# Sparse attention with queries made transposed, a 96-row compressed-value product, and a reordered opening

## The chip, the cores and the metric

One core of a Trainium2 chip runs the kernel. Its engines have queues of their own: TensorE (PE, with its weight loads PEld), VectorE (DVE), ScalarE (ACT), GpSimd (POOL) and SyncE (SP, which here only issues loads). The metric is the time of one execution on the device in microseconds (us); lower is better.

## The reference

Two layers of a decoder on 256 tokens of width 1024, all in fp32. Layer 0 mixes with causal pooling and a gated delta rule, layer 1 with the sparse attention below; each layer then attends to 256 memory tokens and applies a squared-ReLU MLP.

```python
q, kc, vc, ks, vs, kw, vw, gl = split_cols(z, C_SIZES)      # z = rmsnorm(x) @ w_in
ck = compress_kv(kc, ...); cv = compress_kv(vc, ...)        # 15 compressed blocks, 4 groups of 64
...
p_cmp = where(any(ok_c), softmax(q . ck * scale - slope * dist), 0)
o_cmp = einsum('bgrqc,bcgd->bqgrd', p_cmp, cv)
...
o = gb[..., 0:1] * o_cmp + gb[..., 1:2] * o_slc + gb[..., 2:3] * o_win
```

There are 16 query heads of 64 columns in 4 groups; three branches (compressed, selected, window) with their own keys and values are mixed by sigmoid gates.

## The kernel before, in words

**Three-term products.** Every weight arrives in fp32 and is split by `wsplit`: ACT writes the high part `hi` (L187), DVE or POOL the rest `lo` (L188; after a step `sh2` every second split goes to POOL). Activations are split likewise by `evac_hl` (ACT L245 `hh`, DVE L247 or L249 `hl`). `mm3` then multiplies hi by hi, hi by lo and lo by hi (L197 to L199) in fp32r. `block_b` makes a 128-column block of the output transposed (weights stationary, 24 matmuls of 256 columns); `dense_a` makes it with tokens on the partitions (matmuls of up to 512 columns, activations stationary).

**The opening** is in `mixer0`: tokens in two tiles t of 128, the row norm (`norm_act`, `norm_dve`, `norm_pow` L394 and L395, `norm_mul` L399 and L400 writing `cv`), PE transposes (`flip`, L455) into four PSUM tiles `pt` that hold two of the eight blocks k each, their evacuation `evac_x`, and a first product `first_mm` on the weights `a_ba`. `ea` (L493) and `onh` (L494) are two small results from the constants `vec`. A manual schedule keeps this part in the order written.

**The order of the rest** is set by lists of steps (`MIX` for layer 0's mixer, `NSA` for the sparse attention), run one after the other; a scheduler with priorities then places each engine's instructions, and fills with the projections of the memory attention (`k0` to `k8`). In `MIX`, `inv0` and its followers invert 32x32 blocks: ACT copies blocks into `ec` (L598), DVE multiplies by masks (`al`, L605), forms `T` (L609) and transposes it into `bc` (L611), PE multiplies (`blocks32`, L592), ACT takes the result as `Y` (L623).

**The sparse attention** is `nsa`. Steps `q0` and `q1` are two `dense_a` of 512 query columns; `ev_q` scales by the row norm `r` and by a row of constants `qr0` or `qr1` (`qd`, L1143) and splits each head into high and low 64 columns (`qn`, ACT L1148, DVE L1149). Steps `t0` to `t3` transpose these (L1160) and copy them (`qs`, L1162), so that `qs` has a head's high part on partitions 0 to 63 and its low part on 64 to 127. `compress` multiplies by the compression weights (L1080), `s` or `pc` receives its result (L1084); `comp_k` (L1091) and `comp_v` (L1102, L1104) go on from it. Step `s` p (`scores`) treats two heads: products with `vw`-tagged keys (L1177 to L1187), softmax pieces on DVE (L1193, L1199 to L1204). Step `v` p (`values`) transposes the probabilities (L1217 for the compressed branch `Pc`, evacuated to `pcT` at L1218; L1227 to L1229 for the others) and accumulates: L1244 and L1246 on 64-column tiles, then the compressed branch:

```python
            pe.matmul(po[:, :S], CV[g][:64], pcT[:64], start=False, stop=True)
```

`CV` and `pcT` are fp32 there, 64 rows: two heads with 32 rows each, of which 15 hold blocks.

## Time and profile before

| | |
|---|---|
| three runs | 863.91, 864.16, 864.18 us (median 864.16) |
| the profiled execution | 865.69 us, its span 863.9 us |
| busy in the span | PE 847.2, PEld 766.0, DVE 534.3, ACT 500.9, POOL 202.9 us |
| the chain that ended last | PE 89%, DVE 4%, ACT 3% |

The span is the part of an execution that the profiler shows; the execution's own time holds what lies around it. A matmul's busy time counts its latency, and neighbours overlap, so the pitch from start to start says what one costs. Times in the rows are microseconds from the span's start.

### The profile page before, as it was taken

The numbers are of one execution on the slowest core, as the hardware profiler recorded it, in microseconds if no ns is written. First come the engines' busy times: TensorE is split into PE (matmuls) and PEld (weight loads), VectorE is DVE, ScalarE is ACT, GpSimd is POOL, SyncE is SP. The second block draws the span as 40 slices with busy tenths as digits, with TensorE's granted clock in tenths as the row PEclk, the third lists the DMA queues.
The fourth block names the chain that finished last, engine by engine and source line by source line (L and its number), as shares of the span: only waits on it lengthen the run. The fifth ranks groups of instructions, "written<-read, shape, count | busy, mean of one in ns | idle before, by whom it ended". The sixth has DMA issues, their size and how long they took to land.

```text
span 863.9 us, 16134 instructions
## 1 busy us (share of the span) xinstructions
PE 847.2 (98%) x6231; PEld 766.0 (89%) x6231; DVE 534.3 (62%) x1043; ACT 500.9 (58%) x1018; POOL 202.9 (23%) x185
## 2 busy tenths in 40 slices
PE   7999999999999999999999999999999999999997
PEld 5999998899899999999889888888998999999995
DVE  5897657566575555555548797855555755555554
ACT  5896655755475445445676667756554754554452
POOL 0001710400012222222334454443100122222220
PEclk9999999999999999999999999999999999999999
DMA  8643444465546666666644321145545466666641
GB/s 281 191 135 101 137 127 140 156 213 184 158 147 201 189 191 183 191 193 199 203 148 162 125 99 50 51 123 173 167 152 166 147 198 192 189 184 190 191 151 49
DMA packets 41261, 138.77 MB, mean 161 GB/s; under 512 B 4576, under 2 KB 5088, under 8 KB 41184
## 3 DMA queue, kind: packets, MB, share of 16 engines
q1 hardware_dynamic: 40032, 135.69, 50.6%
q10 hardware_dynamic: 1152, 2.05, 0.7%
q8 instruction: 49, 0.80, 0.4%
q14 instruction: 28, 0.23, 0.1%
HBM read 136.67 MB, written 1.05 MB: 159 GB/s over the span
## 4 chain that ended last, share of the span: by engine, by line
PE 89%; DVE 4%; ACT 3%; issue 1%; DMA 1%; SPq 0%; POOL 0%; POOLq 0%; DVEq 0%; ACTq 0%
PE acc L197 12%; PE acc L199 12%; PE acc L198 12%; PE mb L197 10%; PE mb L198 10%; PE mb L199 10%; PE tp L197 4%; PE tp L198 4%; PE tp L199 4%; PE acc L592 1%; PE tp L259 1%; PE tp L1244 1%; DVE lo L188 1%; ACT hi L187 1%; ACT junk L273 1%
## 5 line engine op out<-in xcount | busy, mean ns | idle before, releaser
L187 ACT ACTIVATE hi<-raw 128x1024 fp32r<-128x1024 f32 (+2 forms) x256 | 263.8, 1033 | 252.5 <-PE acc L199 116.8
L188 DVE TENSOR_TENSOR lo<-raw,hi 128x1024 fp32r<-128x1024 f32 (+3 forms) x227 | 277.6, 1225 | 195.4 <-ACT hi L187 194.3
L197 PE MATMUL acc<-hi,hh 128*128 128x512 f32 (+3 forms) x496 | 189.2, 382 | 0.0
L198 PE MATMUL acc<-lo,hh 128*128 128x512 f32 (+3 forms) x496 | 189.0, 381 | 0.0
L199 PE MATMUL acc<-hi,hl 128*128 128x512 f32 (+3 forms) x496 | 188.9, 381 | 0.0
L197 PE MATMUL mb<-hh,hi 128*128 128x256 f32 x640 | 182.1, 285 | 0.6 <-ACT hi L187 0.6
L198 PE MATMUL mb<-hl,hi 128*128 128x256 f32 x640 | 181.1, 284 | 0.0
L199 PE MATMUL mb<-hh,lo 128*128 128x256 f32 x640 | 180.1, 283 | 0.0
L946 POOL TENSOR_TENSOR rs<-rs 128x256 f32<-128x256 f32 x64 | 74.5, 1174 | 238.7 <-ACT rs L944 238.7
L197 PEld LDWEIGHTS mb<-hh,hi 128*128 128x128 f32 x640 | 120.7, 189 | 2.5 <-ACT hi L187 1.1
L198 PEld LDWEIGHTS mb<-hl,hi 128*128 128x128 f32 x640 | 120.9, 189 | 2.2 <-issue 1.0
L199 PEld LDWEIGHTS mb<-hh,lo 128*128 128x128 f32 x640 | 121.2, 190 | 0.1
L199 PEld LDWEIGHTS acc<-hi,hl 128*128 128x128 f32 x496 | 93.5, 189 | 18.4 <-DVE hl L249 0.6
L197 PEld LDWEIGHTS acc<-hi,hh 128*128 128x128 f32 x496 | 93.7, 189 | 17.5
L198 PEld LDWEIGHTS acc<-lo,hh 128*128 128x128 f32 x496 | 93.7, 189 | 17.2
L188 POOL TENSOR_TENSOR lo<-raw,hi 128x1024 fp32r<-128x1024 f32 (+2 forms) x29 | 68.8, 2373 | 93.1 <-ACT hi L187 86.5
L197 PE MATMUL tp<-hh,hi 128*128 128x256 f32 x256 | 72.0, 281 | 0.0
L198 PE MATMUL tp<-hl,hi 128*128 128x256 f32 x256 | 71.7, 280 | 0.0
L199 PE MATMUL tp<-hh,lo 128*128 128x256 f32 x256 | 71.6, 280 | 0.0
L199 PEld LDWEIGHTS tp<-hh,lo 128*128 128x128 f32 x256 | 48.3, 188 | 0.0
L198 PEld LDWEIGHTS tp<-hl,hi 128*128 128x128 f32 x256 | 48.2, 188 | 0.0
L197 PEld LDWEIGHTS tp<-hh,hi 128*128 128x128 f32 x256 | 48.1, 188 | 0.0
...
## 6 DMA issues: line engine op xcount, KB each, us to landing
raw<-in_ff_w_dram SPq DMA_DIRECT2D x128, 512.0 KB, 3.8
...
```

The costliest lines, as they stand in the source:

```text
L187: act.activation(hi[:, :n], raw[:, :n], AF.Copy)
L188: lo_eng.tensor_sub(lo[:, :n], raw[:, :n], f(hi[:, :n]))
L197: pe.matmul(ps, sh, mh, start=start, stop=False)
L198: pe.matmul(ps, sh, ml, start=False, stop=False)
L199: pe.matmul(ps, sl, mh, start=False, stop=stop)
L259: pe.transpose(ps[:, j * S + t * P:j * S + (t + 1) * P], src(t, k0 + j), ident)
L273: act.activation(junk[:, :src.shape[-1]], src, AF.Square, accum_out=accum)
L592: pe.matmul(ps[o, c], lhs[o, c], rhs[o, c], start=True, stop=True)
L946: pool.tensor_tensor(sq, rl, rl, op=ALU.mult)
L1244: pe.matmul(po[rows, :S], v, pts[a][bi][:, :S], start=bi == 0, stop=False)
```

## The change

Queries are made transposed at once: eight `block_b` of 128 columns (two heads) replace the two `dense_a`, the transposes and their copies. `ev_q` scales by a column `qcol` and by `rb`, the row norm along the columns (made by `r_cols` with two products and a copy), ACT writes the high part on the head's own 64 partitions and DVE the low part on the other 64. The compressed values become 96 rows in fp32r: three groups of 32 rows with high part, low part and high part of `CV`, against high, high and low part of `pcT`, one pass. `hp` and `Pc` are written in three copies for that. In the opening `ea` and `onh` come last, the eight blocks are evacuated in the order 0, 2, 1, 3, 4, 6, 5, 7, and the part has a higher priority. `MIX` and `NSA` list their steps in another order.

```diff
...
-NSA = """sh2 kcvc w0 kskw pre0 vs gate kb0 kb1 q0 pre1 vw kb2 ck kb3 t0 t1 s0 w1 k0 q1 cv s1 v0 k1 s2 k2 v1 v2 s3 k3
+NSA = """sh2 kcvc w0 kskw pre0 vs rb gate q0 kb0 kb1 q1 pre1 vw ck kb3 s0 k0 q2 w1 q3 cv kb2
...
-        with tc.manual_schedule(engines={mybir.EngineType.Activation, mybir.EngineType.DVE, mybir.EngineType.PE}):
+        with tc.high_priority(offset=1000), tc.manual_schedule(engines={mybir.EngineType.Activation, mybir.EngineType.DVE, mybir.EngineType.PE}):
...
-            def first_mm(j):
-                for k2 in range(2):
-                    k = 2 * j + k2
-                    h3, l3 = (b3(z[:, :528], 264) for z in us[j])
-                    for t in range(2):
-                        mm3(ps[t][:, :264], tuple(a[:, t * P:(t + 1) * P] for a in hT[k]), (h3[:, k2], l3[:, k2]), k == 0, k == KT - 1)
-            for j in range(4):
-                for k in (2 * j, 2 * j + 1):
+            def first_mm(k):
+                h3, l3 = (b3(z[:, :528], 264) for z in us[k // 2])
+                for t in range(2):
+                    mm3(ps[t][:, :264], tuple(a[:, t * P:(t + 1) * P] for a in hT[k]), (h3[:, k % 2], l3[:, k % 2]), k == 0, k == KT - 1)
+
+            for ks in ((0, 2), (1, 3), (4, 6), (5, 7)):
+                for k in ks:
                     evac_x(pt, k)
-                if j < 2:
-                    us.append(wsplit("a_ba", j + 2, 528))
-                first_mm(j)
+                    if k in (2, 3):
+                        us.append(wsplit("a_ba", k, 528))
+                    first_mm(k)
+            act.activation(ea, V("a_log"), AF.Exp)
+            dve.tensor_scalar(onh, V("o_norm"), 0.5, None, op0=ALU.mult)
...
-        act.activation(ea, V("a_log"), AF.Exp)
-        dve.tensor_scalar(onh, V("o_norm"), 0.5, None, op0=ALU.mult)
...
-        D1, Dc, qr0, qr1 = gt('D1', 1, 528), gt('Dc', 1, 400), gt('qd', 3), gt('qd', 3)
-        for d, o in ((D1, 0), (Dc, 528), (qr0, 928), (qr1, 1440)):
+        D1, Dc = gt('D1', 1, 528), gt('Dc', 1, 408)
+        for d, o in ((D1, 0), (Dc, 528)):
             nc.scalar.dma_start(d, A["cst2"][:, o:o + d.shape[-1]])
-        D0, cblk = Dc[:, :272], Dc[:, 272:]
+        D0, cblk, qcol = Dc[:, :272], Dc[:, 272:400], Dc[:, 400:]
...
-            hp = gt('pc', 2, 256)
+
+            hp = gt('z', 8)[:, :384]
             pool.memset(hp, 0.0)
-            hp4 = hp.rearrange("p (g a b) -> p g a b", g=4, a=2)
-            compress(1, pre[1], w1[1], [hp4[:, :, a, :15] for a in range(2)])
+            compress(1, pre[1], w1[1], [hp.rearrange("p (g c b) -> p g c b", g=4, c=6)[:, :, c, :15] for c in range(6)])
             ps = tp()
             for g in range(4):
-                pe.matmul(ps[:64, g * 64:(g + 1) * 64], hp[:, g * 64:(g + 1) * 64], V("w2_v"), start=True, stop=True)
-            cv = gt('cv', 1)
-            dve.tensor_tensor(cv[:64].rearrange("p (g a d) -> p g a d", g=4, a=2),
-                              b3(ps[:64, :256], 64).unsqueeze(2).to_broadcast([64, 4, 2, 64]),
-                              b3(cblk[:64], 64).unsqueeze(1).to_broadcast([64, 4, 2, 64]), op=ALU.mult)
+                pe.matmul(ps[:96, g * 64:(g + 1) * 64], hp[:, g * 96:(g + 1) * 96], V("w2_v"), start=True, stop=True)
+            cvf, cv = gt('z', 8), gt('cv', 1, 512, F32R)
+            dve.tensor_tensor(cvf[:96].rearrange("p (g a d) -> p g a d", g=4, a=2),
+                              b3(ps[:96, :256], 64).unsqueeze(2).to_broadcast([96, 4, 2, 64]),
+                              b3(cblk[:96], 64).unsqueeze(1).to_broadcast([96, 4, 2, 64]), op=ALU.mult)
+            act.activation(cv[:96], cvf[:96], AF.Copy)
+            dve.tensor_sub(cv[32:64], cvf[32:64], f(cv[32:64]))
             for g in range(4):
-                CV.append(cv[:, g * P:(g + 1) * P])
+                CV.append(cv[:96, g * P:(g + 1) * P])
...
-        Pc = [gt(f"Pc{i}", 1, P).rearrange("p (t a b) -> p t a b", t=2, a=2) for i in range(2)]
-        for z in Pc:
-            pool.memset(z, 0.0)
+        Pc = {}
 
         oT = [None] * 8
-        qn = {}
-
-        def ev_q(c):
-            def ev(t, q, ps):
-                d = gt('qd', 3)
-                dve.scalar_tensor_tensor(d, ps, r[:, t:t + 1], (qr0, qr1)[c], op0=ALU.mult, op1=ALU.mult)
-                for i in range(2):
-                    s = gt('qn', 4, 512, F32R)
-                    s4 = s.rearrange("p (h a d) -> p h a d", h=4, a=2)
-                    d3 = b3(d[:, i * 256:(i + 1) * 256], 64)
-                    act.activation(s4[:, :, 0], d3, AF.Copy)
-                    dve.tensor_sub(s4[:, :, 1], d3, f(s4[:, :, 0]))
-                    qn[2 * c + i, t] = s
-            return ev
-
         qs = {}
         ek = {}
-
-        def q_t(g):
+        rb = gt('rb', 1, S)
+
+        def r_cols():
+
+            ps = tp()
             for t in range(2):
-                ps = tp()
-                for h in range(4):
-                    pe.transpose(ps[:, h * P:(h + 1) * P], f(qn[g, t][:, h * P:(h + 1) * P]), ident)
-                qs[g, t] = gt('qs', 4, 512, F32R)
-                act.activation(qs[g, t], ps, AF.Copy)
+                pe.matmul(ps[:, t * P:(t + 1) * P], r[:, t:t + 1].to_broadcast([P, P]), ident, start=True, stop=True)
+            act.activation(rb, ps[:, :S], AF.Copy)
+
+        def ev_q(p, ps):
+
+            d = gt('qd', 3, S)
+            dve.scalar_tensor_tensor(d, ps, qcol[:, p:p + 1], rb, op0=ALU.mult, op1=ALU.mult)
+            s = gt('qs', 8, 512, F32R)
+            u, v = slice(0, 64), slice(64, 128)
+            for rows, other, c in ((u, v, slice(0, S)), (v, u, slice(S, 2 * S))):
+                act.activation(s[rows, c], d[rows], AF.Copy)
+                dve.tensor_sub(s[other, c], d[rows], f(s[rows, c]))
+            qs[p] = s
...
-            pc = Pc[p % 2]
+            pc = small([P, 2, 2, 16], "pcp", 2)
             for t in range(2):
                 for a in range(2):
-                    h = (2 * p + a) % 4
-                    st = qs[g, t][:, h * P:(h + 1) * P]
+                    st = qs[p][:, a * S + t * P:a * S + (t + 1) * P]
...
-            pc = pc[:, :, :, 0:16]
...
-            dve.tensor_tensor(pc, pc, rs[:, :, :, 0:1].to_broadcast([P, 2, 2, 16]), op=ALU.mult)
+            Pc[p] = gt('Pc', 2, 192).rearrange("p (t c a b) -> p t c a b", t=2, c=3, a=2)
+            for t in range(2):
+                dve.tensor_tensor(Pc[p][:, t], pc[:, t].unsqueeze(1).to_broadcast([P, 3, 2, 16]),
+                                  rs[:, t, :, 0:1].unsqueeze(1).to_broadcast([P, 3, 2, 16]), op=ALU.mult)
...
-            pcT = gt('pc', 2, 256)[:, :S]
+            pcT = gt('pc', 2, S, F32R)
             ps = tp()
             for t in range(2):
-                pe.transpose(ps[:64, t * P:(t + 1) * P], Pc[p % 2][:, t].rearrange("p a b -> p (a b)"), ident)
-            act.activation(pcT[:64], ps[:64, :S], AF.Copy)
+                pe.transpose(ps[:96, t * P:(t + 1) * P], Pc[p][:, t].rearrange("p c a b -> p (c a b)"), ident)
+
+            act.activation(pcT[:96], ps[:96, :S], AF.Copy)
+            dve.tensor_sub(pcT[64:96], ps[64:96, :S], f(pcT[64:96]))
...
-            pe.matmul(po[:, :S], CV[g][:64], pcT[:64], start=False, stop=True)
+            pe.matmul(po[:, :S], CV[g], pcT[:96], start=False, stop=True)
...
```

ACT's queue in the opening, before (`junk` are the sums of squares, `cv` the normalised tokens, `hi` the split of `a_ba`, `hh` the evacuated blocks; `tp_136` and `tp_137` are two PSUM tiles):

```order
L493 ACTIVATE ea_360<-vec 128x4
L400 ACTIVATE cv_124<-x_83,n_0_8_127 128x512
L187 ACTIVATE hi_158<-raw_93 128x528
L400 ACTIVATE cv_126<-x_85,n_0_8_127 128x512
L187 ACTIVATE hi_172<-raw_93 128x528
L245 ACTIVATE hh_178<-tp_136,vec 128x256
L245 ACTIVATE hh_182<-tp_136,vec 128x256
L187 ACTIVATE hi_186<-raw_97 128x528
L245 ACTIVATE hh_202<-tp_137,vec 128x256
L245 ACTIVATE hh_206<-tp_137,vec 128x256
```

and now:

```order
L400 ACTIVATE cv_124<-x_83,n_0_8_127 128x512
L187 ACTIVATE hi_159<-raw_93 128x528
L400 ACTIVATE cv_126<-x_85,n_0_8_127 128x512
L187 ACTIVATE hi_173<-raw_93 128x528
L245 ACTIVATE hh_179<-tp_137,vec 128x256
L245 ACTIVATE hh_189<-tp_138,vec 128x256
L187 ACTIVATE hi_193<-raw_97 128x528
L245 ACTIVATE hh_203<-tp_137,vec 128x256
L245 ACTIVATE hh_213<-tp_138,vec 128x256
```

`ea` has left its place ahead of the normalisation, and neighbouring evacuations read different PSUM tiles.

DVE's queue in layer 0's mixer, ahead of the first `bc` that L592 reads, before:

```order
L605 TENSOR_TENSOR al_748<-ec_743,cst 128x128
L605 TENSOR_TENSOR al_748<-ec_743,cst 128x512
L609 TENSOR_TENSOR T_750<-cst,al_748 128x128
L424 SCALAR_TENSOR_TENSOR cv_741<-ct_734 128x256
L611 STREAM_TRANSPOSE bc_752<-T_750 128x128
```

and now:

```order
L605 TENSOR_TENSOR al_748<-ec_743,cst 128x128
L417 SCALAR_TENSOR_TENSOR ct_734<-ct_734,vec 128x253
L609 TENSOR_TENSOR T_750<-cst,al_748 128x128
L605 TENSOR_TENSOR al_748<-ec_743,cst 128x512
L611 STREAM_TRANSPOSE bc_752<-T_750 128x128
```

`cv` of L424 no longer stands ahead of `bc`; it now comes five rows behind it.

PE's queue in the sparse attention, from the last products on the compression of the keys (L1080) to what follows L1091, before (the 512-column products are the second half of the queries):

```order
L1080 MATMUL tp_5718<-z_5419,kk_5316 128x60 x4
L197 MATMUL mb_5882<-hi_5886,hh_5110 128x512
L198 MATMUL mb_5882<-lo_5887,hh_5110 128x512
...
L198 MATMUL mb_5883<-lo_5887,hh_5110 128x512
L199 MATMUL mb_5883<-hi_5886,hl_5111 128x512
L1091 MATMUL tp_5738<-s_1088_5716,vec 128x64
L1113 MATMUL tp_5748<-cst,z_5401 128x128
L1113 MATMUL tp_5748<-cst,z_5397 128x128
L1113 MATMUL tp_5748<-cst,z_5395 128x128
L1113 MATMUL tp_5748<-cst,z_5399 128x128
L197 MATMUL mb_5883<-hi_5886,hh_5114 128x512
L198 MATMUL mb_5883<-lo_5887,hh_5114 128x512
```

and now (L1115 is the former L1113, L1172 and L1173 are scores):

```order
L1080 MATMUL tp_5692<-z_5412,kk_5309 128x60 x4
L197 MATMUL mb_5829<-hh_5110,hi_5825 128x256
L198 MATMUL mb_5829<-hl_5111,hi_5825 128x256
...
L199 MATMUL mb_5829<-hh_5123,lo_5826 128x256
L197 MATMUL mb_5829<-hh_5127,hi_5825 128x256
L1091 MATMUL tp_5712<-s_1077_5690,vec 128x64
L1115 MATMUL tp_5722<-cst,z_5394 128x128
L1115 MATMUL tp_5722<-cst,z_5390 128x128
L1115 MATMUL tp_5722<-cst,z_5388 128x128
L1115 MATMUL tp_5722<-cst,z_5392 128x128
L1172 MATMUL acc_5735<-vw_5212,qs_5534 128x272
L1173 MATMUL acc_5735<-vw_5216,qs_5534 128x272
```

Ten products of 256 columns stand between L1080 and L1091 where nine of 512 did, and the first scores come right behind the four transposes.

## Rows read from the trace of the kernel before

**Rows 1.** The profile's page: busy time of each engine; the chain's shares.
```profile
PE 847.2 (98%) x6231; PEld 766.0 (89%) x6231; DVE 534.3 (62%) x1043; ACT 500.9 (58%) x1018; POOL 202.9 (23%) x185
...
PE 89%; DVE 4%; ACT 3%; issue 1%; DMA 1%; SPq 0%; POOL 0%; POOLq 0%; DVEq 0%; ACTq 0%
```
**Rows 2.** Windows: length; busy PE, PEld, DVE, ACT, POOL; PE clock; DMA share; GB/s.
```profile
18.00:50.00 32.00, 31.70 (x266) 31.41 (x267) 28.42 (x60) 26.54 (x65) 0.00 (x0) 1.00 0.67 214
50.00:62.00 12.00, 10.78 (x118) 10.56 (x116) 10.97 (x32) 11.87 (x31) 1.65 (x1) 1.00 0.31 91
62.00:66.00 4.00, 4.00 (x46) 3.78 (x46) 3.20 (x8) 3.00 (x7) 0.00 (x0) 0.57 0.00 0
487.00:560.00 73.00, 71.81 (x557) 61.88 (x559) 59.20 (x298) 56.21 (x190) 33.84 (x33) 1.00 0.20 66
```
**Rows 3.** Waits in 0 to 24 us: total, times, longest.
```profile
PE tp L455 <- DVE cv L399: 4.6, 2, 3.2
...
ACT hh L245 <- DVE hl L249: 3.8, 4, 1.7
```
**Rows 4.** Timeline of DVE in the opening: start, duration, instruction.
```profile
5.68 0.16 DVE L394 TENSOR_TENSOR n<-n,n 128x1 f32<-128x1 f32 x1
8.20 0.15 DVE L494 TENSOR_SCALAR onh<-vec 128x1 f32<-128x1 f32 x1 [2.36 <-DMA vec<-in_vec_dram]
8.29 0.49 DVE L399 TENSOR_SCALAR cv<-x,n 128x512 f32<-128x512 f32 x1
...
23.20 0.48 DVE L249 SCALAR_TENSOR_TENSOR hl<-acc,vec,hh 128x256 fp32r<-128x256 f32 x1 [0.54 <-ACT hh L245]
```
**Rows 5.** The chain in 56 to 62 us: start, share of time, instruction.
```profile
60.35 0.42 DVE cv L424
...
61.14 0.87 PE acc L592 x32
```
**Rows 6.** Waits of PE in 435 to 575 us.
```profile
PE tp L1091 <- DVE s L1084: 0.9, 1, 0.9
...
PE tp L1102 <- DVE pc L1084: 0.5, 1, 0.5
```
**Rows 7.** Timeline of PE around a compressed-value product.
```profile
509.03 0.39 PE L1246 MATMUL tp<-pt,vv 128*64 128x128 f32 x4
509.35 0.70 PE L1247 MATMUL tp<-pc,cv 64*128 64x256 f32 x2
509.97 0.39 PE L1184 MATMUL acc<-vw,qs 128*128 128x256 f32 x1
```
**Rows 8.** The chain in 470 to 540 us, four pieces.
```profile
490.02 0.23 PE mb L199
...
503.65 0.12 PE mb L198
...
509.20 0.22 PE tp L1246 x4
...
527.14 0.87 PE tp L1160 x8
```
**Rows 9.** The line L550: minimum, median and maximum ns, first and last start.
```profile
L550 PE MATMUL acc<-cst,ld x16: 272/275/356, 45.1 to 48.2; 128*128 128x128 f32 x16
```
**Rows 10.** Groups of DVE by shape, 435 to 575 us: busy, mean ns, idle before.
```profile
L247 DVE TENSOR_TENSOR hl<-tp,hh 128x256 fp32r<-128x256 f32 x8 | 3.4, 422 | 4.5 <-ACT hh L245 4.5
...
L1204 DVE TENSOR_TENSOR Pc<-Pc,nrs 128x64 f32<-128x64 f32 x8 | 1.8, 221 | 0.1
...
L1143 DVE SCALAR_TENSOR_TENSOR qd<-mb,rstd,qd 128x512 f32<-128x512 f32 x2 | 1.4, 738 | 0.0
```
**Rows 11.** The tile `qn` on DVE.
```profile
L1149 DVE TENSOR_TENSOR qn<-qd,qn x8: 411/416/2628, 468.7 to 501.4; 128x256 fp32r<-128x256 f32 x8
```
**Rows 12.** Timeline of POOL, in the opening and near 497 us.
```profile
6.00 0.55 POOL L395 TENSOR_TENSOR n<-n,mhalf 128x1 f32<-128x1 f32 x1 [5.17 <-DVE n L394]
...
497.12 3.38 POOL L188 TENSOR_TENSOR lo<-raw,hi 128x1024 fp32r<-128x1024 f32 x1
```

More of the change, by code (lines that the diff above doesn't have):

```diff
@@ L60 @@
 _n = 0
-for _name, _w in [("D1", 528), ("D0", 272), ("cblk", 128), ("qrow", D)]:
+for _name, _w in [("D1", 528), ("D0", 272), ("cblk", 128), ("qcol", 8)]:
     CST2[_name] = (_n, _w)
@@ L433, in mixer0 @@
         onh = small([P, 1], "onh", 1)
+        ea = small([P, 4], "ea", 1)
         GO = [gt('GO', 2) for _ in range(2)]
@@ L487, in mixer0 @@
         sh = [P, 2, 4]
-        beta, y, e, u1, ln, ld, ea = (small(sh if s != "ea" else [P, 4], s, 1) for s in ("beta", "y", "e", "u1", "ln", "ld", "ea"))
+        beta, y, e, u1, ln, ld = (small(sh, s, 1) for s in ("beta", "y", "e", "u1", "ln", "ld"))
         act.activation(beta, ba[:, :, 0:4], AF.Exp, scale=-1.0)
@@ L1253, in nsa @@
                 "vs": lambda: dense_a(hT, "c_vsgl", 0, 304, ev_vsgl, acc),
-                "vw": lambda: dense_a(hT, "c_vw", 0, 256, ev_vw, acc), "ck": comp_k, "cv": comp_v,
-                "q0": lambda: dense_a(hT, "c_q", 0, 512, ev_q(0), acc), "q1": lambda: dense_a(hT, "c_q", 1, 512, ev_q(1), mb)}
-        for s, f_, w in (("w", w1_load, 2), ("pre", comp_pre, 2), ("kb", k_build, 4), ("t", q_t, 4), ("s", scores, 8), ("v", values, 8)):
+                "vw": lambda: dense_a(hT, "c_vw", 0, 256, ev_vw, acc), "ck": comp_k, "cv": comp_v, "rb": r_cols}
+        for s, f_, w in (("w", w1_load, 2), ("pre", comp_pre, 2), ("kb", k_build, 4), ("q", lambda p: block_b(hT, "c_q", p, ev_q), 8), ("s", scores, 8), ("v", values, 8)):
             step.update((f"{s}{i}", lambda i=i, f_=f_: f_(i)) for i in range(w))
@@ L1342, in pack @@
     r["c_vw"] = ua(w[:, 2304:2560])
[L1343 removed]
+    r["c_q"] = ub(w[:, :1024])
     for s in "kv":
@@ L1403, in pack @@
     o, n = CST2["cblk"]
-    c[:, o:o + n] = 0.5 * np.repeat(np.arange(P)[:, None] // 32 == np.arange(2)[None], 64, 1)
-    o, n = CST2["qrow"]
-    c[:, o:o + n] = np.repeat(np.array([0.125 / s for s in SLOPES]), 64)[None]
+    c[:, o:o + n] = 0.5 * np.repeat(np.arange(P)[:, None] // 16 % 2 == np.arange(2)[None], 64, 1)
+    o, n = CST2["qcol"]
+    c[:, o:o + n] = np.repeat(np.array([0.125 / s for s in SLOPES]).reshape(8, 2).T, 64, 0)
     r["cst2"] = c
```

7 lines of the change are left out of this document (3 added, 4 removed).

## The prediction

> **What bounds the kernel now.** I first read the busy shares and the chain that ended last [rows 1]. TensorE (PE) is busy for 847.2 of 863.9 us and makes 89% of the chain. So a change is worth what it takes out of PE's own instructions, plus what it takes out of PE's few waits, and work of other engines counts only where PE waits for it. The windows [rows 2] show where that can be: in 18 to 50 us PE works 31.70 of 32, in 487 to 560 us 71.81 of 73, and in 50 to 62 us 10.78 of 12, while ScalarE (ACT) is at 11.87 of those 12. [...]
>
> Then the waits of the opening [rows 3]: PE's first transposes (L455) wait 4.6 us for VectorE's (DVE) normalisation `cv`, and ACT waits 3.8 us for DVE's low parts `hl`. DVE's timeline [rows 4] shows why: the sum of squares (L394) is complete at 5.84 us, but `onh` of L494 stands next in DVE's queue and waits 2.36 us for the load of `vec`, so the normalisation, whose factor POOL has computed from 6.00 to 6.55 [rows 12], waits behind it. The chain through layer 0's mixer [rows 5] shows the second place: just before PE's first L592 at 61.14, ACT's tanh (L419) has just ended when DVE's `cv` (L424) runs, 0.42 us from 60.35, and only behind it comes the transpose `bc` (L611), which L592 reads. In the sparse attention PE has two waits worth naming [rows 6]: 0.9 us at L1091 for `s` and 0.5 us at L1102 for `pc`.
>
> **The change, part by part.**
>
> *PE's work in the sparse attention.* What counts is the pitch from one matmul's start to the next's; a matmul's own 0.28 to 0.4 us is its latency. In the chain, which gives each its pitch, one of 256 columns takes 0.12 us and one of 512 takes 0.23 [rows 8].
> - The 32 query transposes of L1160 go. Eight of them take 0.87 us in the chain [rows 8], so 3.5 us for all.
> - The dense query product has the same number of columns, 96 of 512 against 192 of 256: by these rounded pitches 192 x 0.12 - 96 x 0.23 = +1.0, by equal columns 0; I take +0.4 us.
> - The compressed product (L1247) was two records of 64 rows: the first starts at 509.35 and the next instruction at 509.97, 0.62 us [rows 7]. The new one is one pass over 256 columns, so by the pitch 0.12: 8 x 0.50 = 4.0 us. From below: the four L1246 ahead of it take 0.32 us (509.03 to 509.35), where the chain gives four of them 0.22 [rows 8]; this 0.10 may be paid at a change of tile shape, and the new 128-column tile still stands behind 64-column ones. If the new product pays it on both sides, 8 x (0.62 - 0.12 - 0.20) = 2.4. From above: the 0.10 goes too, 4.8. [...] I take 4.0, in the middle.
> - `r_cols` adds two 128x128 fp32 products. L550 is that kind, with 16 records of 0.275 us [rows 9]; two products are 4 records, at a pitch of 0.11 to 0.28 each: +0.4 to +1.1, I take +0.5.
>
> Sum: -3.5 + 0.4 - 4.0 + 0.5 = **-6.6 us, from -4.9 to -7.4**. PE is the bound here, so this should arrive whole, less what the next part gives back.
>
> *PE's waits in the sparse attention.* The wait at L1102 (0.5) goes: in the new order 29 three-term products and score matmuls stand between `pc` and the product that reads it. The wait at L1091 stays: ahead of it stood nine products of 512 columns (2.1 us), now ten of 256 (1.2 us), while DVE has a similar amount to do; I expect 0.8 to 1.3 us. Behind it now only four transposes (0.44 us) stand ahead of the first scores, which read the compressed keys that ACT and DVE have yet to write: a new wait of 0.3 to 0.5.
>
> More may come from DVE. Its prices [rows 10]: added are eight `qd` of 128x256 (a little over half of the 0.74 for 512 columns: 0.45, 3.6 us), 16 subtractions of 64x256 (0.42 each as for 128x256, 6.7 us), 16 products of 96 columns for `Pc` (0.25 each, a little above the 0.22 of 64 columns: 4.0 us), eight `pcT` (0.42, 3.4 us) and about 1.2 us in `comp_v`. Removed are four `qd` (2.9), eight `qn` (seven at 0.42 and one at 2.63 [rows 11], 5.5) and eight L1204 (1.8). Net +9 us. In 487 to 560 us DVE is busy for 59.20 of 73 [rows 2]: 13.8 us free. Six of the eight query blocks now fall into that stretch, and with them weight splits that used to lie ahead of it, so that more than the net, 8 to 14 us, comes to it, while PE's saving makes it some 5 us shorter. DVE is then at 93% or more, close behind PE, and a hand-over that is late there is a wait of PE's: the query block's `qd` is first in DVE's queue where scores and weight splits wait behind it. I put 0.8 us on that, with nothing as the low end (the old work came in lumps of four `qd` and eight `qn`, which are gone) and 4 us as the high one. Wait change in all, with L1091, L1102 and the first scores: **+1.2 us, from -1 to +4.5**.
>
> *Other engines.* ACT loses eight copies of 128x512 and gains 16 of 64x256; it isn't the bound there, and the cover is PE's dense work.
>
> *The opening.* With `onh` and `ea` behind, `cv` can start at about 6.6 instead of at 8.29 us: 1.7 us earlier. The new order of evacuations takes `hh` and `hl` from two different PSUM tiles in turn, so that ACT no longer waits for DVE to have read the same tile: most of the 3.8 us of [rows 3]. I follow both queues with the durations of the trace: the first product (L197) starts 1.6 us earlier, and all eight pairs are there at about 17.3 us, where the last `hl` ended at 23.7 before [rows 4]. PE's stalls and early start add up to **3.9 us** of work done ahead at 20 us.
>
> *How much of that survives.* At 50 to 62 us ACT is saturated [rows 2], and its chain sets the first L592. ACT has one weight split (0.95 us) less ahead of the `ec` that L592 needs, one `pk` (0.2) more, and DVE's `bc` no longer stands behind `cv` of L424, which waited for the tanh: 0.42 of DVE plus a few tenths [rows 5]. So ACT and DVE get there 1.3 us earlier even without the opening. But PE comes to it with 15 products (1.8 us) fewer done. Before, PE waited 1.2 us there (12 - 10.78 in [rows 2]). Without any of the opening's gain passed on to ACT: 1.3 - 1.8 = 0.5 us lost, and the 3.9 us is spent as a longer wait. With all of it passed on: 3.4 to 3.9 us kept. ACT had 5.5 us of idle time in 18 to 50 us [rows 2], which were waits for PE and for loads; the first kind shrinks with the opening, the second only if raw buffers come free earlier. I take half: **-2.0 us, from -4.5 to +1**. [...]
>
> Total: -6.6 + 1.2 - 2.0 = **-7.4 us**. Against the profiled execution's own time of 865.69 us that is 858.3; the runs timed have a median 1.5 us lower, 864.16, so the prediction is **856.8 us**.
>
> **Rivals.**
> - *The opening's gain is carried whole.* ACT's waits in 18 to 44 us are mostly for PE, so its chain moves with it. Then -6.6 + 1.2 - 3.9 = -9.3: 854.9. Against it speaks that ACT is saturated from 44 us on, and that a load stands in the chain ahead.
> - *The opening's gain is lost whole* to the longer wait at the first L592: -6.6 + 1.2 + 0.5 = -4.9: 859.3. For it speaks that ACT's work alone decides that time, against it that ACT's work ahead is smaller.
> - *DVE becomes the bound in the sparse attention,* and PE waits 4 us more than I count: 860.8. For it speaks that DVE comes to 93% or more of the stretch, against it that 487 to 560 us already had DVE at 81% and PE lost only 1.2 us.
> - *Slower than before.* Each new 64-row subtraction reads two SBUF tensors, as `qn` did, and of the eight `qn` one took 2.63 us where the median is 0.416 [rows 11]; the trace puts it at 498.15, inside a weight split that POOL ran from 497.12 for 3.38 us [rows 12]. If all 16 took 2.63 us, DVE would need 16 x 2.2 = 35 us more, and with about 3 us of slack left PE would wait for 32: 889. Slower begins where 3 + 7.4 + 1.7 = 12 us more are needed, at an average of 0.42 + 12/16 = 1.2 us. Against it: seven of eight did not, and the mean of the eight was 0.69. [...]
>
> **How the numbers follow.** Within 0.2% (1.7 us) of before counts as no change. Chances: forecast (partial carry) 0.52; carried whole 0.14; lost whole 0.15; DVE-bound 0.13; slower 0.03; what I don't see 0.03. The range takes in the forecast, the two beside it with the bounds of the compressed product, and DVE-bound: 853.0 to 861.2. Faster 0.92; the same 0.05 (lost whole and DVE-bound together come to 863); slower 0.03.
>
> **What would show it.** The chain's share of transposes falls, and the 0.62 us in front of the evacuation of `values` becomes 0.12 to 0.22. `cv` of L399 starts near 6.6 us. PE's wait at the first L592 is 1.5 to 3 us, in `acc <- DVE bc`. If that wait is below 1 us or above 4 us, the carry is mis-sized. If PE's waits for DVE in 475 to 560 us exceed 5 us, DVE is the bound. If PE's busy time falls by less than 4 us from 435 us on, the work sum is wrong.

## The result, and the profile after

The changed kernel is slower, and its runs lie far apart: 863.09, 864.77, 868.99, 870.85 and 874.34 us against 863.91 to 864.18 before, a ratio of 1.0051 (1.0028 to 1.0075). Each run lists the mean clock that TensorE was granted, and the time follows it: 0.996 in the run of 863.09 us, 0.994 in 864.77, 0.988 in 868.99, 0.984 in 870.85, 0.982 in 874.34. So the question is in two parts: what the change does at full clock, and why it loses the clock. The profile is of the run of 864.77 us, so it shows little of what the three slower runs lost; e1 below, with the same opening and mixer, was profiled in a run of 868.19 us. It answers [rows 1] with:

```profile
PE 842.4 (98%) x6291; PEld 767.1 (89%) x6291; DVE 549.3 (64%) x1076; ACT 500.3 (58%) x1020; POOL 203.1 (24%) x183
...
PE 86%; DVE 6%; ACT 4%; issue 1%; DMA 1%; POOL 0%; POOLq 0%; DVEq 0%; ACTq 0%
```

PE's busy time fell by 4.8 us, and the chain has moved from PE to DVE by two to three per cent of the span. The windows that answer to [rows 2], and two more:

```profile
18.00:50.00 32.00, 31.44 (x268) 31.04 (x267) 28.68 (x68) 27.50 (x69) 1.65 (x1) 1.00 0.60 195
50.00:62.00 12.00, 10.21 (x139) 9.84 (x140) 10.39 (x26) 10.35 (x29) 0.00 (x0) 0.86 0.30 87
62.00:66.00 4.00, 4.00 (x117) 3.65 (x113) 2.61 (x7) 3.25 (x9) 2.22 (x2) 1.00 0.58 147
62.00:88.00 26.00, 26.00 (x605) 23.79 (x600) 21.86 (x52) 17.03 (x44) 7.70 (x11) 1.00 0.28 84
487.00:560.00 73.00, 68.97 (x560) 62.38 (x558) 66.46 (x300) 53.23 (x174) 36.72 (x34) 0.98 0.22 68
510.00:520.00 10.00, 8.12 (x58) 7.26 (x57) 8.10 (x33) 4.70 (x19) 4.76 (x4) 0.83 0.42 149
```

In 487 to 560 us DVE is busy for 66.46 us where it was for 59.20, 91% of the stretch, and PE idles for 4.0 us where it idled for 1.2. The third column from the end is the granted clock: in this run it falls after two waits of PE, which end at 56 and at 513 us, to 0.50 in 57 to 60 and in 515 to 517 us, and from 62 to 88 us it stays at 1.00. The first of the two waits is the one at the first product of 32x32:

```profile
56.45 0.74 PE L592 MATMUL acc<-bc,al 32*32 32x32 f32 x20 [1.79 <-DVE bc L611]
```

**The opening** came as forecast or better. `cv` starts at 6.49 us (before: 8.29), waiting for POOL alone:

```profile
5.59 0.16 DVE L394 TENSOR_TENSOR n<-n,n 128x1 f32<-128x1 f32 x1
6.49 0.49 DVE L399 TENSOR_SCALAR cv<-x,n 128x512 f32<-128x512 f32 x1 [0.74 <-POOL n L395]
```

The first product (L197) starts at 10.62 us (before: 12.91; 1.6 us earlier was forecast), and the last `hl` ends at 16.65 (before: 23.68; forecast 17.3). Part of this may be the clock, which the prediction left out here. In 8 to 18 us it was 0.83 in the profiled run of the kernel before and 1.00 in that of the changed one:

```profile
8.00:18.00 10.00, 7.46 (x42) 6.57 (x42) 7.02 (x15) 7.10 (x13) 0.99 (x1) 0.83 0.86 318
```
```profile
8.00:18.00 10.00, 8.33 (x66) 7.76 (x65) 8.70 (x17) 8.22 (x16) 0.92 (x1) 1.00 1.03 377
```

**PE's waits in the sparse attention**, 435 to 580 us, beside the two of [rows 6] and one of 0.6 that made 2.0 us in all:

```profile
PE tp L1226 <- DVE pt L1233: 2.1, 2, 1.9
PE tp L1243 <- DVE pt L1233: 1.4, 1, 1.4
PE tp L1055 <- DVE vw L247: 1.2, 2, 0.7
PE tp L1226 <- DVE hl L247: 1.2, 1, 1.2
PE tp L1091 <- DVE s L1084: 1.1, 1, 1.1
PE tp L1226 <- DVE vw L247: 0.5, 1, 0.5
PE tp L1226 <- DVE pc L1217: 0.3, 1, 0.3
```

They come to 7.8 us, all for DVE. The longest shows how: on DVE a query block's subtraction and a weight split stand ahead of the copy `pt` that frees the PSUM tile for PE's next transposes,

```profile
510.58 0.47 DVE L1157 TENSOR_TENSOR qs<-qd,qs 64x256 fp32r<-64x256 f32 x1
511.08 1.46 DVE L188 TENSOR_TENSOR lo<-raw,hi 128x1024 fp32r<-128x1024 f32 x1
512.57 0.56 DVE L1233 COPY pt<-tp 128x384 f32<-128x384 f32 x1
```

and PE, whose last product started at 511.12, waits until that copy has ended:

```profile
513.28 0.30 PE L1226 MATMUL tp<-cst,z 128*128 128x128 f32 x1 [1.88 <-DVE pt L1233]
```

**The compressed product**, against [rows 7]:

```profile
500.93 0.39 PE L1245 MATMUL tp<-pt,vv 128*64 128x128 f32 x4
501.25 0.38 PE L1246 MATMUL tp<-pc,cv 96*128 96x256 f32 x1
501.47 0.28 PE L198 MATMUL mb<-hl,hi 128*128 128x256 f32 x1
```

The product takes 0.22 us instead of 0.62, and the four ahead of it still take 0.32: 8 x 0.40 = 3.2 us saved, not 4.0. (L1245 and L1246 are the former L1246 and L1247.)

### The profile page after: what moved, and what is told of

Its sections match the earlier page's. It is cut to its first block, busy times and chain, and to the rows that moved or that the text cites. A ratio compares the mean times of both kernels' runs of the same rounds, so it can differ in the third digit from the quotient of the medians.

```text
span 863.0 us, 16267 instructions
## 1 busy us (share of the span) xinstructions
PE 842.4 (98%) x6291; PEld 767.1 (89%) x6291; DVE 549.3 (64%) x1076; ACT 500.3 (58%) x1020; POOL 203.1 (24%) x183
## 4 chain that ended last, share of the span: by engine, by line
PE 86%; DVE 6%; ACT 4%; issue 1%; DMA 1%; POOL 0%; POOLq 0%; DVEq 0%; ACTq 0%
PE acc L197 12%; PE acc L199 12%; PE acc L198 12%; PE mb L197 10%; PE mb L198 10%; PE mb L199 10%; PE tp L197 4%; PE tp L198 4%; PE tp L199 4%; PE acc L592 1%; DVE lo L188 1%; PE tp L259 1%; ACT hi L187 1%; ACT junk L273 1%; PE tp L1243 1%
## 5 line engine op out<-in xcount | busy, mean ns | idle before, releaser
L197 PE MATMUL mb<-hh,hi 128*128 128x256 f32 x704 | 200.8, 286 | 0.4 <-ACT ct L415 0.4
L198 PE MATMUL mb<-hl,hi 128*128 128x256 f32 x704 | 199.2, 284 | 0.0
L199 PE MATMUL mb<-hh,lo 128*128 128x256 f32 x704 | 198.2, 282 | 0.0
L199 PE MATMUL acc<-hi,hl 128*128 128x512 f32 (+3 forms) x480 | 182.4, 380 | 0.3 <-DVE hl L249 0.3
L197 PE MATMUL acc<-hi,hh 128*128 128x512 f32 (+3 forms) x480 | 182.6, 380 | 0.0
L198 PE MATMUL acc<-lo,hh 128*128 128x512 f32 (+3 forms) x480 | 182.3, 380 | 0.0
L198 PEld LDWEIGHTS mb<-hl,hi 128*128 128x128 f32 x704 | 133.5, 190 | 1.2 <-DVE hl L249 0.4
L197 PEld LDWEIGHTS mb<-hh,hi 128*128 128x128 f32 x704 | 133.2, 190 | 1.5 <-ACT ct L415 0.6
L199 PEld LDWEIGHTS mb<-hh,lo 128*128 128x128 f32 x704 | 133.5, 190 | 0.2
L197 PEld LDWEIGHTS acc<-hi,hh 128*128 128x128 f32 x480 | 90.3, 188 | 17.0 <-ACT hh L245 0.3
L197 PE MATMUL tp<-hh,hi 128*128 128x256 f32 x256 | 72.0, 281 | 0.0
L197 PEld LDWEIGHTS tp<-hh,hi 128*128 128x128 f32 x256 | 48.1, 188 | 0.0
```

The source lines that it names most:

```text
L197: pe.matmul(ps, sh, mh, start=start, stop=False)
L198: pe.matmul(ps, sh, ml, start=False, stop=False)
L199: pe.matmul(ps, sl, mh, start=False, stop=stop)
```

## Experiments

The theory at first was that DVE had become the bound in the sparse attention and that its waits brought the slower clock; the rival, that layer 0's mixer did. Ratios are to the kernel before, with 95% intervals. Where an expectation speaks of 1.2 GHz, no run shows a frequency: what the traces show is a granted clock of 0.50 (62.5 to 65.5 us of the kernel before), at which products of 256 columns start 0.21 us apart, where at 1.00 they start 0.12 apart (53.8 to 55.8 us).

### The parts apart

**e1** has the new opening and `MIX` alone, **e2** the rest alone:

```diff
-MIX = """g1 kn1 q0 kn0 cum q1 kr e1 e0 v0 i0 q2 i1 inv1 v1 v2 q3 inv2 inv3 mem v3 k0 inv4 vn0 inv5 u0 et1 u1 u2 pk u3 et0 k1 k2 pw qn0 qn1
+MIX = """g1 cum kn1 q0 kn0 q1 kr e1 e0 v0 i0 q2 i1 v1 inv1 v2 inv2 q3 inv3 mem v3 inv4 k0 et0 vn0 et1 inv5 u0
...
```

> The kernel before with the new opening and the new order of layer 0's mixer alone; the sparse attention as before. Theory (DVE became the bound in the sparse attention, PE's longer waits there also bring TensorE to 1.2 GHz in a number of stretches that differs from run to run): the sparse attention is untouched, so 860 to 862.5 us, runs within 1 us of each other. Rival 1 (the longer wait at the first L592 in layer 0's mixer is what lowers the clock): 864 to 870 us, with runs 5 us or more apart.

> The sparse attention's part of the change alone, with opening and layer 0's mixer as before. Theory: median 866 to 873 us, runs 5 us or more apart, as the whole change shows. Rival 1: 859 to 862 us, runs within 1 us of each other.

Measured: e1 867.00 us (860.87 to 869.18), 1.0023 (1.0006 to 1.0040); e2 864.60 us (864.15 to 865.85), 1.0008 (0.9999 to 1.0016). The theory fell on both: the spread belongs to the opening and the mixer. For e1 the rival's range held, though e6 and e13 below show that the wait it names (1.7 us in e1's profile) is not what costs most; for e2 its 859 to 862 us did not come either, since the sparse attention, with its waits unchanged at 7.8 us, costs 0.6 us. So its work term and its waits all but cancel. The profile of e1 shows where the opening and the mixer lose the clock:

```profile
62.00:88.00 26.00, 26.00 (x489) 23.61 (x484) 17.75 (x44) 14.49 (x36) 5.90 (x7) 0.74 0.18 59
```

That is 26 x 0.26 = 6.8 us, in a stretch in which PE shows as busy throughout.

**e5** has the new opening alone and **e6** the new `MIX` alone.

> The kernel before with the new opening alone, layer 0's mixer in its old order. Theory (the new order of layer 0's mixer, with 15 products less ahead of the inversions of 32x32 blocks, is what brings TensorE to 1.2 GHz in 66 to 82 us; the opening itself gains): 861 to 863 us, runs within 1 us of each other, clock 1.00 in 66 to 82 us. Rival (the earlier opening brings it, by a longer wait at the first L592): 864 to 869 us, runs 5 us or more apart.

> The kernel before with the new order of layer 0's mixer alone, opening as before. Theory: 864 to 870 us, runs 5 us or more apart, some of them with clock 0.5 in 66 to 82 us. Rival: 863 to 865 us, runs within 1 us.

Measured: e5 862.03 us (860.91 to 867.65), 0.9976 (0.9950 to 1.0002), 7 of 12 runs below 862.3; e6 876.95 us (873.28 to 878.25), 1.0125 (1.0085 to 1.0165). The median of e5 is as forecast, its spread of 6.7 us is not, and the profile of its run of 867.65 us has a clock of 0.80 in 62 to 88 us, with the mixer in its old order:

```profile
62.00:88.00 26.00, 26.00 (x542) 24.58 (x536) 19.31 (x46) 15.08 (x38) 2.54 (x3) 0.80 0.28 84
```

e6 lies above both ranges: the order of the mixer's steps costs 13 us by the medians and 11 by the ratio, more than the whole change. The kernel before is not free of this either: of its 128 runs made beside these experiments, six took 867.96 to 874.77 us, at mean clocks of 0.978 to 0.989. Windows of e6 (busy PE, PEld, DVE, ACT, POOL, then the clock):

```profile
62.00:88.00 26.00, 25.51 (x410) 23.55 (x410) 17.36 (x37) 12.47 (x30) 4.40 (x5) 0.54 0.18 55
88.00:106.00 18.00, 18.00 (x259) 16.44 (x258) 11.53 (x25) 9.43 (x24) 3.82 (x11) 0.72 0.40 107
```

PE shows as busy for 25.51 of 26 us, yet at a clock of 0.54: 26 x 0.46 + 18 x 0.28 = 17 us are lost in this run of 878.25 us. Waits do not explain it; in 50 to 110 us e6 has one line for PE, with the same 1.2 us that PE waited at L592 before:

```profile
PE acc L592 <- DVE bc L611: 1.2, 2, 0.7
```

What differs is what PE does there. Counted in the traces, 94 products of 256 columns stand between the first 32x32 product (L592) and the last (L670) before, 80 in the changed kernel and 66 in e6. The tile of a 32x32 product is a sixteenth of the 128x128 tile of these full-size products. What the clock follows is not shown: the profile's busy share, 25.51 of 26 us here, is near one at a clock of 0.54.

**e14** moves `cum` alone, **e15** everything of `MIX` but `cum`.

```diff
-MIX = """g1 kn1 q0 kn0 cum q1 kr e1 e0 v0 i0 q2 i1 inv1 v1 v2 q3 inv2 inv3 mem v3 k0 inv4 vn0 inv5 u0 et1 u1 u2 pk u3 et0 k1 k2 pw qn0 qn1
+MIX = """g1 cum kn1 q0 kn0 q1 kr e1 e0 v0 i0 q2 i1 inv1 v1 v2 q3 inv2 inv3 mem v3 k0 inv4 vn0 inv5 u0 et1 u1 u2 pk u3 et0 k1 k2 pw qn0 qn1
```

> The kernel before with one step of layer 0's mixer moved as in the change: cum to second place. Between its first and last 32x32 product the full-size rows are grouped 8, 4, 21, 8, 1, 31, 15 (before: 15, 1, 14, 8, 3, 8, 21, 29, 6, 9 with other counting of transposes). Theory (the change of the inversions' neighbours is what costs the clock): 863 to 866 us. Rival (the earlier cum does it): 870 us or more.

> The kernel before with the new mixer order except that cum keeps its old place. Theory: the inversions follow one another with little full-size work between (groups 15, 1, 5, 3, 6, 7, 33), so the clock falls as with the whole new order: 870 to 878 us. Rival (the earlier cum does it): 863 to 866 us.

Measured: e14 867.59 us (865.44 to 870.07), 1.0042 (1.0022 to 1.0062); e15 866.88 us (864.06 to 872.41), 1.0030 (1.0010 to 1.0050), five runs of 12 below 864.5 and six above 868. Neither half carries it alone, so both expectations failed: each moves products out from among the inversions (80 and 63 stand there, where there were 94), and together they cost more than the sum of 3.6 and 2.8.

The number alone does not rank the kernels. e15 has the fewest and keeps the clock in five runs (its profile, of the run of 864.36 us, has 1.00 from 62 to 106 us); e5 has 97, more than the kernel before, and loses the clock in five. Where the products stand differs too, although e5 has the old list of steps: in its trace 27 stand in the gap between the groups of 32x32 products that ends at 66.7 us, and 0, 5, 1 and 5 in the next four, to 73.5 us. In the kernel before, 1, 14, 8 and 3 stand in the gaps from 66 to 74 us. In e5's profile the clock is 1.00 up to 72 us and 0.50 behind it, and PE shows as busy throughout:

```profile
70.00:72.00 2.00, 2.00 (x67) 1.70 (x65) 1.37 (x5) 0.00 (x0) 0.00 (x0) 1.00 0.00 0
72.00:74.00 2.00, 2.00 (x26) 1.72 (x23) 1.01 (x3) 0.58 (x2) 0.00 (x0) 0.50 0.04 8
```

### Filling the inversions

**e11** and **e13** add products that nobody reads to e6; in e13, whose edit is shown, they read `bc` or `Y`, which holds them directly ahead of the 32x32 products.

```diff
+        def fill(ps, z):
+            for _ in range(2):
+                pe.matmul(ps[:, 256:384], z[:, :P], ident, start=True, stop=True)
...
                 yp = acc()
+                fill(yp, B[t])
                 blocks32(yp, Am[t][:, l * P:(l + 1) * P], B[t])
```

> The kernel before with the new order of layer 0's mixer, and with 32 products of 128x256 added that nobody reads, 26 of them among the 32x32 products (66 full-size products stand there with the new order, 94 with the old one). They cost 3.7 us at full clock. Theory: the clock stays up, so the kernel with more work is faster than without: 866 to 871 us instead of 877. Rival (the 1.2 GHz stretch has another cause, such as the waits at the first L592): 879 to 882 us.

> The kernel before with the new mixer order, and two fp32 products of 128x128 that nobody reads directly ahead of each of the 16 groups of 32x32 products, held there by their operand (7 us of added work at full clock, and a longer chain). Theory (full-size work among the 32x32 products keeps the clock up): less of 62 to 104 us at 1.2 GHz than the 33 us without the filling, and 867 to 873 us, faster than 877 with less work. Rival (what is lost there does not hang on full-size work): 882 us or more.

Measured: e11 877.57 us (871.06 to 883.64), 1.0162 (1.0121 to 1.0204): outside both ranges. The scheduler put eight of its products ahead of the first inversion, the next groups stayed as bare as before, and although 94 full-size products then stand among the 32x32 ones, the clock in its profile is 0.93 in 62 to 88 us and 0.81 in 88 to 106. So this run does not separate the two, and it speaks against the number alone. e13 873.62 us, all four runs within 0.35 us, 1.0107 (1.0089 to 1.0125), above the forecast and below the rival's range. It has some 7 us more work than e6 (32 products of two records at 0.11) and a median 3.3 us lower; but one run of e6, 873.28 us, was as fast, and the two intervals overlap, so that the times alone show no gain. The clock does: 0.994 or 0.995 in its four runs, against 0.976 to 0.985 in the six of e6. Its windows, and its one line of waits for PE in 50 to 110 us:

```profile
62.00:88.00 26.00, 25.80 (x499) 23.45 (x499) 20.35 (x44) 13.91 (x36) 5.17 (x5) 1.00 0.33 103
88.00:106.00 18.00, 18.00 (x281) 16.93 (x277) 9.67 (x21) 10.29 (x25) 5.78 (x15) 1.00 0.21 66
```
```profile
PE acc L619 <- DVE bc L611: 0.9, 2, 0.7
```

The clock is 1.00 in all of it, with nearly the same waits (0.9 us, in e6 1.2). So what e6 loses in the mixer is not due to these waits: with full-size work directly ahead of every group of 32x32 products, the same order keeps the clock. How little of it would do, no run shows.

### The waits of the sparse attention

**e3** is the whole change with the old compressed product, **e4** the kernel before with the new one.

> The whole change with the compressed product as before (64 rows in fp32, one copy of Pc, no low part of pcT). DVE has 7 us less to do in the sparse attention, PE 4 us more. Theory: PE's waits there fall by 5 us or more from about 13, the clock drops less often, median 859 to 866 us. Rival 2 (not the amount of DVE's work but the new order of steps makes PE wait): the waits stay at 11 or more, median 868 us or more.

> The kernel before with the 96-row product alone (queries and all orders as before). DVE has 7 us more to do in the sparse attention, PE 4 us less. Theory: PE's waits there grow by 2 to 6 us, so 862 to 866 us. Rival 2: the old order stands, waits as before, 860 us.

Measured: e3 869.35 us (ten runs from 863.92 to 873.85, one of 877.99), 1.0048 (1.0024 to 1.0071), named waits 7.0 us; e4 864.48 us (864.23 to 865.10), 1.0004 (0.9996 to 1.0013), named waits 4.9. Without the new product's DVE work the waits are nearly the same in the new order (7.0 against 7.8), and with it alone they grow by 2.9 in the old order, which takes nearly all of its 3.2 us. e4 is as its theory had it; of e3 neither range of waits came. The 13 to 14 us of waits that the expectations of e3, e7 and e10 start from are too high: in 435 to 580 us PE idles for 7.9 us in e2 and in the changed kernel.

**e7** takes the copies of `Pc` from DVE to ACT, **e8** leaves out the subtraction for `pcT`; both start from e2.

```diff
-                dve.tensor_tensor(Pc[p][:, t], pc[:, t].unsqueeze(1).to_broadcast([P, 3, 2, 16]),
-                                  rs[:, t, :, 0:1].unsqueeze(1).to_broadcast([P, 3, 2, 16]), op=ALU.mult)
+                for a in range(2):
+                    act.activation(Pc[p][:, t, :, a], pc[:, t, a].unsqueeze(1).to_broadcast([P, 3, 16]), AF.Copy, scale=rs[:, t, a, 0:1])
```

```diff
-            dve.tensor_sub(pcT[64:96], ps[64:96, :S], f(pcT[64:96]))
```

> The sparse attention's part alone, with the three copies of Pc written by ACT instead of DVE (3.6 us less for DVE). Theory (DVE is the bound in the sparse attention): PE's waits there fall from about 14 us by 3, so 861 to 863 us. Rival (the order of steps, or a chain through ACT too, makes PE wait): 864 to 866 us.

> The sparse attention's part alone, without the subtraction that makes the low part of pcT (this leaves the third group of 32 rows with the high part, so the compressed branch is not the reference's); 3.4 us less for DVE and nothing added elsewhere. Theory: as with the copies on ACT, 3 us less than 864.6: 861 to 863 us. Rival: 864 to 865 us.

Measured: e7 867.18 us (866.37 to 872.16), 1.0030 (1.0005 to 1.0054), waits 8.8; e8 862.98 us (862.61 to 863.44), 0.9975 (0.9954 to 0.9995), waits 5.8. Taking 3.4 us from DVE's path gives 2.0 us of waits back; e8 is as forecast. Giving as much to ACT makes it worse than either range said; the transposes of `values`, which waited for DVE's copies `pt` in e2, now wait for ACT's:

```profile
PE tp L1226 <- ACT pt L1231: 2.1, 3, 1.4
```

**e10** is e2 with the query blocks early; **e9** is the whole change with the old `MIX`, and **e12** is e9 with the query blocks early; **e16** is e12 with the low parts of every second head on POOL.

```diff
-NSA = """sh2 kcvc w0 kskw pre0 vs rb gate q0 kb0 kb1 q1 pre1 vw ck kb3 s0 k0 q2 w1 q3 cv kb2
+NSA = """sh2 kcvc w0 kskw pre0 vs rb gate kb0 kb1 q0 q1 q2 q3 pre1 vw kb2 ck kb3 s0 w1 k0 q4 q5 q6 q7 cv s1 v0 k1 s2 k2 v1 v2 s3 k3
...
-                dve.tensor_sub(s[other, c], d[rows], f(s[rows, c]))
+                (pool if c.start else dve).tensor_sub(s[other, c], d[rows], f(s[rows, c]))
```

> The sparse attention's part alone, with its steps in an order near the old one: the query blocks q0 to q3 ahead of the compression and q4 to q7 right behind the first scores, where the two dense query products stood. The amount of DVE's work is the same. Theory now (the order, with a query block's DVE work between scores and values, makes PE wait): PE's waits from 450 to 575 us fall from 14 to 9 us or less, 859 to 862.5 us. Rival (the amount of DVE's work): waits 12 us or more, 863.5 to 866 us.

> The whole change, but with layer 0's mixer in its old order. Theory (the new mixer order leaves fewer full-size products among the 32x32 products, and TensorE runs at 1.2 GHz there in many runs): the clock stays up in 62 to 88 us in most runs; opening -2.0 and sparse attention +0.6 add up: 862 to 863 us median. Rival (the slower clock belongs to the opening or to the sum of all parts): 866 us or more.

> New opening, old mixer order, and the sparse attention with the query blocks early. Theory: the gains of the opening (2.0) and of the early order (2 to 4) add up: 858 to 860.5 us. Rival: 863 us or more.

> New opening, old mixer order, query blocks early, and the low parts of every second head made by POOL instead of DVE (DVE 4 us less). Theory (the amount of DVE's work is the other half of the waits): PE's named waits from 435 to 580 us fall from 4.6 to 3 us or less, 860 to 862 us. Rival (DVE and POOL hold each other up, or POOL is late): waits 5 us or more, 863 to 866 us.

Measured: e10 863.34 us (862.91 to 864.87), 0.9990 (0.9977 to 1.0002), named waits 4.8; e9 863.79 us (862.25 to 867.71), 0.9996 (0.9987 to 1.0004), waits 8.1; e12 862.87 us (860.27 to 865.87), 0.9988 (0.9977 to 1.0000), waits 4.6; e16 862.60 us (860.71 to 865.38), 0.9975 (0.9952 to 0.9998), waits 4.3. The order of the steps is 3.0 us of the 5.8 that the waits grew by. With the old `MIX` the whole change is level with the kernel before. All four missed the times forecast, e10 although its waits fell as forecast. In e9, e12 and e16 some runs still lose the clock; e12 would have missed without that too, since its seven runs with a mean clock of 0.996 or more took 860.27 to 863.13 us. Moving 4 us from DVE to POOL gave only 0.3, which is not clear of the spread.

### Real work instead of added work

**e17** is e16 and **e18** is e5, each with one step moved, so that 16 products that came behind `inv3` come ahead of it:

```diff
-MIX = """g1 kn1 q0 kn0 cum q1 kr e1 e0 v0 i0 q2 i1 inv1 v1 v2 q3 inv2 inv3 mem v3 k0 inv4 vn0 inv5 u0 et1 u1 u2 pk u3 et0 k1 k2 pw qn0 qn1
+MIX = """g1 kn1 q0 kn0 cum q1 kr e1 e0 v0 i0 q2 i1 inv1 v1 v2 q3 inv2 v3 inv3 mem k0 inv4 vn0 inv5 u0 et1 u1 u2 pk u3 et0 k1 k2 pw qn0 qn1
```

> New opening, query blocks early, POOL for the low parts of every second head, and the old mixer order with one step moved: v3 ahead of inv3, so that 16 full-size products that stood behind the inversions now stand between them. No work is added. Theory (full-size work among the 32x32 products keeps the clock up): runs within 1.5 us of each other, no 1.2 GHz in 62 to 88 us, 860 to 861.5 us. Rival: runs spread as without the move (860.7 to 865.4), median 862.5 us or more.

> The kernel before with the new opening and the same step moved, v3 ahead of inv3; the sparse attention as before. Theory: 860.9 to 861.8 us and within 1.5 us of each other, where the new opening alone gave 860.9 to 867.7. Rival: spread as without the move.

Measured: e17 861.45 us (860.49 to 862.68), 0.9971 (0.9960 to 0.9983); e18 861.24 us (860.71 to 862.64), 0.9972 (0.9961 to 0.9984). Both beat the kernel before. Their medians are in the ranges forecast, and the spread is 2 us, a little more than the 1.5 forecast. In e18's trace 2, 5 and 17 full-size products stand in the three gaps from 65 to 70.5 us, where e5 has the bare ones; from the first to the last 32x32 product there are 102 in place of 97. The mean clock is 0.999 in all six runs of e18, where it was 0.990 to 0.999 in e5. Of the 13 runs of e17 and e18 none is above 862.68 us, of the 24 of e5 and e16 ten are above 863.3. But these 13 were made on another chip, on which all 12 runs of the kernel before were within 0.7 us of each other, so that a part of the difference may be the chip's. The windows of a single run do not show it: e17, below, has 1.00 in both, and so has the profile of e16, of a run of 861.18 us.

```profile
62.00:88.00 26.00, 26.00 (x562) 24.01 (x562) 21.35 (x51) 17.44 (x44) 7.21 (x14) 1.00 0.33 103
88.00:106.00 18.00, 17.34 (x150) 16.46 (x148) 10.48 (x13) 11.52 (x33) 14.63 (x25) 1.00 0.51 162
```

The times of e17 and e18 are equal: the opening gives all of the gain, and the sparse attention, at its best here, gives none that can be measured.

How far each kernel is when the sparse attention's first transposes load (L1055: minimum, median, maximum ns, first and last start) tells the first part by itself; in this order the kernel before, the changed one, e6 and e17:

```profile
L1055 PEld LDWEIGHTS tp<-cst,z x16: 138/141/142, 448.8 to 469.3; 128*128 128x128 f32 x16
```
```profile
L1055 PEld LDWEIGHTS tp<-cst,z x16: 138/140/144, 446.5 to 463.6; 128*128 128x128 f32 x16
```
```profile
L1055 PEld LDWEIGHTS tp<-cst,z x16: 137/141/143, 461.4 to 481.9; 128*128 128x128 f32 x16
```
```profile
L1055 PEld LDWEIGHTS tp<-cst,z x16: 138/140/144, 444.6 to 466.5; 128*128 128x128 f32 x16
```

The profiled run of the kernel before lost 1.7 us in the stretch of [rows 2] at a clock of 0.57 (62 to 66 us). By its time, 865.69 us against a median of 863.99, most of its runs did not; e4, whose first part is the same, has a clock of 1.00 in 62 to 66 us and is there at 446.9.

## Why the prediction was wrong

**The step that failed** is "How much of that survives", with its bounds. It gave the opening and the mixer -2.0 us from -4.5 to +1. The low end counted the slow stretch of [rows 2] as gone, 4 us at a clock of 0.57 and so 1.7 us; the high end allowed for a second one at the same price. The stretch is not one more of the same: with the new order it takes most of 62 to 88 us and part of 88 to 106 (clocks of 0.54 and 0.72, 17 us lost in the profiled run of e6), and how much of it comes differs from run to run. I took the idle time ahead of the stretch of [rows 2] as what had lowered the clock, and so looked at the order of steps only for who waits for whom. Idle time may play a part: in the profiled run of the changed kernel the clock fell right behind the wait of 1.79 us, to 0.50 from 57 to 60 us. But the larger loss comes where PE shows as busy, and in these runs it hangs on the full-size work among the 32x32 products, of which the change left 80 products where 94 stood, and on where that work stands. e6 (13 us from the order alone) and e13 (clock 1.00 with a filling, at nearly the same waits) show this for the new order; e17 and e18 (spread of 2 us when real products are put there) agree for the old one. For the three slow runs of the changed kernel itself it is inferred from e1, since none of them was profiled. The 1.8 us of fewer products ahead of the first L592 stood in my sum as a longer wait only; that wait did come (1.79 us, chain `bc`, at 56.45 us; forecast 1.5 to 3).

**The opening itself** gained what was forecast for it: -2.0 us in e5, and -2.6 in e18, against 3.9 us of work ahead, of which half was to survive. That the numbers agree is partly luck. The forecast of -2.0 was for the opening together with the new order of the mixer, which cost e1 3.0 us instead; and the clock of 1.00 in 8 to 18 us, which e5 and e18 have too, was no term of it.

**PE's work in the sparse attention** was right in kind and too large by a tenth: the compressed product gave 3.2 us instead of 4.0. It takes 0.22 us (501.25 to 501.47), 0.10 more than the pitch of 0.12 that the sum put on it, and 8 x 0.10 is the 0.8 that is missing. The other terms were not measured one by one.

**PE's waits in the sparse attention** were mis-sized: forecast +1.2 us from -1 to +4.5 (the terms named there add up to +0.9), measured 7.8 against 2.0, +5.8. They are all for DVE; in 475 to 560 us they come to 4.9, just short of the mark of 5 that was set, and the rest lies on both sides of that stretch. In size this is the rival in which DVE becomes the bound: 4.6 us more than counted, where it had 4. L1091 (1.1), with 0.8 to 1.3 forecast, and the end of the L1102 wait were right, and the wait of 0.3 to 0.5 at the first scores did not come; what I had not counted are 1.2 us at L1055 and the 5.5 us of `values`' transposes and products (L1226, L1243) behind query blocks and weight splits in DVE's queue. By the runs about half of the growth is the order of steps (e10: 4.8); the rest may be the amount of DVE's work, which e4 and e8 show to count. DVE's added work was two us more than worked out: 11.2 instead of 9 in 435 to 580 us (116.7 against 105.5 busy). The 16 subtractions have a median of 0.42 us and a maximum of 1.31:

```profile
L1157 DVE TENSOR_TENSOR qs<-qd,qs x16: 418/420/1312, 460.6 to 537.3; 64x256 fp32r<-64x256 f32 x16
```

Two of them began while POOL ran a weight split, and both ended just behind it. They are the first of the pair at 482.10 us, with 1.31 us, and the one at 514.06, with 0.98; POOL's splits end at 483.13 and 514.76:

```profile
482.10 1.76 DVE L1157 TENSOR_TENSOR qs<-qd,qs 64x256 fp32r<-64x256 f32 x2
514.06 0.98 DVE L1157 TENSOR_TENSOR qs<-qd,qs 64x256 fp32r<-64x256 f32 x1
```
```profile
480.71 2.42 POOL L188 TENSOR_TENSOR lo<-raw,hi 128x1024 fp32r<-128x1024 f32 x1 [7.49 <-ACT hi L187]
511.88 2.88 POOL L188 TENSOR_TENSOR lo<-raw,hi 128x1024 fp32r<-128x1024 f32 x1
```

The other 14 met no split. So two of the 16 were late as the one `qn` of [rows 11] had been, but at a mean of 0.51 us the subtractions are far from the 1.2 at which the slower rival would have begun; it was not what made the kernel slower.

**Net.** Sparse attention: about 5.8 us of work saved by the terms as corrected, 5.8 lost in waits, and in some runs a stretch at a lower clock behind the longest of them (0.83 over 510 to 520 us, 10 x 0.17 = 1.7 us, in the profiled run of e2 as well). That gives 0 without the stretch and +1.7 with it. e2 measured +0.2 to +0.6 in the seven runs with a mean clock of 0.994 to 0.997 and +1.4 to +1.9 in the four with 0.992, so the sum is right to about 0.5 us. Opening and mixer: -2.0 and +13 apart, +3.0 together (e1). The two parts come to +3.6, the whole change to +5.0 in five runs that lie 11 us apart. The range of the prediction has a low end, 853.0, that its terms do not give (854.9 less 0.8 is 854.1); nothing hung on that.

What stays open: how much full-size work is enough, and where; whether the bare gaps in e5's trace are all that makes the clock fall in some of its runs (e18 speaks for it, with the reserve of the other chip); why the same kernel keeps the clock in one run and loses it in the next; and what of the 4.3 us of waits left in e16 the order could still take away.
